# Values of two heads in one block of 512 columns: a projection's blocks are widened in a fused two-branch layer

## The chip, the cores and the metric

The kernel runs on one core of one Trainium2 chip. The metric is the device time of one execution, in microseconds (us), as the median of several runs. The engines are named as the profile names them: PE (TensorE, matmuls; PEld is its weight loads), DVE (VectorE), ACT (ScalarE), POOL (GpSimd), SP (SyncE, which issues most transfers).

## The reference, cut to what matters

The layer has 1024 positions of width 1024. The input is normalised and modulated to `h`, and one projection of `h` gives everything that the two branches need:

```python
h = rms_norm(x, norm_w[l]) * (1.0 + scale[:, None, :]) + shift[:, None, :]
proj = h @ w_in[l]
hq, hf, hi, hz, gq, gk, gv, gz, ga, mg = jnp.split(proj, IN_OFFSETS, axis=-1)
y_h = hgrn2_branch(hq, hf, hi, hz, lb_all[l], hgrn_norm_w[l])
y_g = gla_branch(gq, gk, gv, gz, ga, gla_alpha_w[l], gla_alpha_b[l], gla_norm_w[l])
...
merged = mg[:, :, 0] * u_h + mg[:, :, 1] * u_g
x = x + gate[:, None, :] * (merged @ w_out[l])
return rms_norm(x, final_norm_w)
```

`gla_branch` (the first branch in the kernel) has 4 heads with keys of width 128 and values `gv` of width 256. Each head is a causal linear attention with a decay per key channel, followed by a norm over the head's 256 values and a gate `silu(gz)`. `hgrn2_branch` (the second) has 8 heads of 128. All products are wanted at nearly full float32 precision.

## The kernel before, in words

Matrix products run on operands split in two rounded halves (`hi`, `lo`, made by one ACT copy, L196, and one DVE subtraction, L197), with three matmuls for each product: hi x hi, hi x lo and lo x hi. `h` is kept as eight pairs of tiles 128x1024 (`h_hi`, `h_lo`), columns by positions.

The middle of the program is a list of jobs (`Stream.jobs`), each one block of the input projection. A `Feat` job makes 128 columns of the projection, channels on the partitions (48 matmuls of 512 positions, L541): the gates z, some keys k, and the second branch's q and f. A value job makes positions on the partitions: its stationary operand is 128 positions of `h`, and the moving one is the weights. `Vblk` (L566) makes the 256 value columns of one first-branch head: 192 matmuls of 256 columns (L600 to L602), evicted in two pieces of 128x1024. `Vblk2` (L610) makes 512 columns: 192 matmuls of 512 (L643 to L645), evicted in four pieces. Before the change only the second branch uses `Vblk2`, where 512 columns are four heads.

`Stream.go` runs the jobs in order. A job yields after each unit of work: a `Feat` job 8 times (6 matmuls each), `Vblk` 16 times (12 each), `Vblk2` 32 times (6 each). After every unit `weave` advances two side tracks by fixed amounts: the heads' attentions (`side`, one after another, first in first out) and a back track (`back`: factors and weight sums for the last products, later the output gate). In this way the order of a head's matmuls among the projection's is set by counts of units. `Stream.ahead` loads the weights of up to two jobs ahead and splits those of one job ahead, as far as free buffers allow. Buffers are 46 slots of 128x1024 (`Slots`), taken and given back in turn; a transfer into a slot waits on the chip until the slot's last reader is done, and SP works its queue in order. The back track starts a weight sum only when 12 slots are free (L1185).

A first-branch head (`attention`, L657) makes its scores in three groups on PE (L683; L715; L770, L776, L781) into one PSUM tile, with DVE work between them; then it transposes the keys (L807), builds running states (L829 and DVE L835), and makes its outputs (L848, L850). A head's attention is put on the side track when its value job is done.

After recording, a scheduler places the instructions on each engine. The jobs of the first branch, before: z, z and values of head 0; the same of head 1; k, z, z and values of head 2; the same of head 3. Then follows the second branch, and then the gated and output products (L1343, L1520).

Of the kernel before, what the change touches and what calls it, by code (L numbers as in the profile page):

```python
# [10 lines left out]
F32R = mybir.dt.float32r  # L11
# [4 lines left out]
P = 128  # L16
D = 1024
T = 1024
KT = D // P
# [5 lines left out]
C_GQ, C_GK, C_GV, C_GZ, C_GA, C_MG = 4096, 4608, 5120, 6144, 7168, 7184  # L25
# [58 lines left out]
def hybrid_trunk_kernel(  # L84
# [6 lines left out]
    nc = tc.nc  # L91
    x2, o2 = x[0], out[0]
    w_in2 = w_in[0]
# [7 lines left out]
    S = Slots(sp, N_SLOTS)  # L101
# [3 lines left out]
    def dtile():  # L105
        cnt[0] += 1
        return ps_d.tile([P, T], F32, tag="d", name=f"pd{cnt[0]}")
# [75 lines left out]
    h_hi = [S.get([T], F32R) for _ in range(KT)]  # L183
    h_lo = [S.get([T], F32R) for _ in range(KT)]
# [6 lines left out]
    def split(src, hi=None, lo=None):  # L191

        if hi is None:
            hi = S.get(list(src.shape[1:]), F32R)
            lo = S.get(list(src.shape[1:]), F32R)
        nc.scalar.copy(hi, src)  # L196
        nc.vector.tensor_sub(lo, src, hi.bitcast(F32))  # L197
        return hi, lo
# [109 lines left out]
    raws = {}  # L308
# [15 lines left out]
    g_state = {}  # L324
# [195 lines left out]
    def load_feat(src, w=P):  # L520

        raw = S.get([KT, P])
        nc.sync.dma_start(raw[:, :, 0:w], src.rearrange("(k p) f -> p k f", p=P))
        return raw, w

    def split_feat(lw):
        raw, w = lw
        hi = S.get([KT, P], F32R)
        lo = S.get([KT, P], F32R)
        split(raw[:, :, 0:w], hi[:, :, 0:w], lo[:, :, 0:w])  # L530
        S.free(raw)
        return hi, lo

    def mm_feat(wt, rhs, ps, w=P):
        hi, lo = wt
        for k in range(KT):
            n = 0
            r_hi, r_lo = rhs(k)
            for a, b in ((hi, r_hi), (hi, r_lo), (lo, r_hi)):
                for th in range(2):  # L540
                    nc.tensor.matmul(ps[0:w, th * 512:(th + 1) * 512], a[:, k, 0:w],  # L541
                                     b[:, th * 512:(th + 1) * 512],
                                     start=(k == 0 and n == 0), stop=(k == KT - 1 and n == 2))
                n += 1
            yield

    class Feat:

        raws, parts = 1, 2

        def __init__(self, src, rhs, done, w=P):
            self.src, self.rhs, self.done, self.w = src, rhs, done, w

        def load(self):
            self.lw = load_feat(self.src, self.w)

        def prep(self):
            self.wt = split_feat(self.lw)

        def run(self):  # L560
            ps = dtile()
            yield from mm_feat(self.wt, self.rhs, ps, self.w)
            S.free(*self.wt)
            self.done(ps)

    class Vblk:  # L566

        raws, parts = 2, 4

        def __init__(self, col, done):  # L570
            self.col, self.done = col, done

        def load(self):
            self.raw = []
            for kk in range(2):
                b = S.get([4, 256])
                nc.sync.dma_start(b, w_in2[kk * 512:(kk + 1) * 512, self.col:self.col + 256].rearrange(
                    "(k p) f -> p k f", p=P))
                self.raw.append(b)

        def prep(self):
            self.wt = []
            for b in self.raw:
                hi = S.get([4, 256], F32R)
                lo = S.get([4, 256], F32R)
                split(b, hi, lo)
                self.wt.append((hi, lo))
                S.free(b)

        def run(self):  # L590
            v = [S.get([4, 256]) for _ in range(2)]
            for g in range(2):
                ps = dtile()
                for i in range(4):
                    t = g * 4 + i
                    for k in range(KT):
                        hi, lo = self.wt[k // 4]
                        lh, ll = h_hi[k][:, t * P:(t + 1) * P], h_lo[k][:, t * P:(t + 1) * P]
                        o = ps[:, i * 256:(i + 1) * 256]
                        nc.tensor.matmul(o, lh, hi[:, k % 4, :], start=(k == 0), stop=False)  # L600
                        nc.tensor.matmul(o, lh, lo[:, k % 4, :], start=False, stop=False)  # L601
                        nc.tensor.matmul(o, ll, hi[:, k % 4, :], start=False, stop=(k == KT - 1))  # L602
                        if k % 4 == 3:
                            yield
                nc.scalar.copy(v[g].rearrange("p a b -> p (a b)"), ps)
            for hi, lo in self.wt:
                S.free(hi, lo)
            self.done(v)

    class Vblk2:  # L610

        raws, parts = 4, 8
# [16 lines left out]
                S.free(b)  # L629

        def run(self):
            v = [S.get([2, 512]) for _ in range(4)]
            for g in range(4):
                if g == 2:
                    self.middle()
                ps = dtile()
                for i in range(2):
                    t = 2 * g + i
                    o = ps[:, i * 512:(i + 1) * 512]
                    for k in range(KT):  # L640
                        hi, lo = self.wt[k // 2]
                        lh, ll = h_hi[k][:, t * P:(t + 1) * P], h_lo[k][:, t * P:(t + 1) * P]
                        nc.tensor.matmul(o, lh, hi[:, k % 2, :], start=(k == 0), stop=False)  # L643
                        nc.tensor.matmul(o, lh, lo[:, k % 2, :], start=False, stop=False)  # L644
                        nc.tensor.matmul(o, ll, hi[:, k % 2, :], start=False, stop=(k == KT - 1))  # L645
                        if k % 2:
                            yield
                nc.scalar.copy(v[g].rearrange("p a b -> p (a b)"), ps)
            for hi, lo in self.wt:
                S.free(hi, lo)  # L650
            self.done(v)
# [257 lines left out]
    J = stream.jobs  # L909


    alphas = {}
# [36 lines left out]
    def silu_done(store, key):  # L949
        def f(ps):  # L950
            s = S.get([T])
            nc.scalar.activation(s, ps, AF.Sigmoid)
            nc.vector.tensor_mul(s, s, ps)
            store[key] = s
        return f
# [13 lines left out]

    def gla_attention(h):  # L970
        qk = g_state
        v = qk.pop(("v", h))
        g = {}
        sq = {}

        def post(vh, half, po):
            if half == 0:
                g[vh] = qk.pop(("z", h, vh))
                sq[vh] = S.get([T])
            sl = slice(half * 512, half * 512 + 512)  # L980
            nc.scalar.activation(sq[vh][:, sl], po, AF.Square)
            nc.vector.scalar_tensor_tensor(g[vh][:, sl], po, vec[:, R_GN + vh:R_GN + vh + 1],
                                           g[vh][:, sl], ALU.mult, ALU.mult)

        yield from attention(qk.pop(("q", h)), qk.pop(("k", h)), alphas[h], lambda: v, 0, 256, post)
        S.free(*v)
        nc.gpsimd.tensor_add(sq[0], sq[0], sq[1])
        yield 1.5
        rst = sq[1]
        yield from inverse_root(rst, sq[0], 256)  # L990
        for half in range(4):
            sl = slice(half * 256, half * 256 + 256)
            for vh in range(2):
                nc.vector.tensor_mul(g[vh][:, sl], g[vh][:, sl], rst[:, sl])
            yield 1.5
        for vh in range(2):
            put_act(yg_d, 2 * h + vh, g[vh])
        S.free(*sq.values())

    def gla_k_done(h):  # L1000
        def f(ps):
            t = S.get([T])
            nc.vector.tensor_copy(t, ps)
            g_state[("k", h)] = t
        return f

    def col(c0, w=P):
        return w_in2[:, c0:c0 + w]

    def start_side(gen, wait=1):  # L1010
        stream.side.append([gen, wait])

    class First:
        raws, parts = 0, 0
# [13 lines left out]
                yield  # L1028

    J.append(First())  # L1030
    for h in range(4):
        if h >= 2:
            J.append(Feat(col(C_GK + h * P), rhs_h, gla_k_done(h)))
        J.append(Feat(col(C_GZ + h * 256), rhs_h, silu_done(g_state, ("z", h, 0))))
        J.append(Feat(col(C_GZ + h * 256 + P), rhs_h, silu_done(g_state, ("z", h, 1))))

        def v_done(v, h=h):
            g_state[("v", h)] = v
            start_side(gla_attention(h))
        J.append(Vblk(C_GV + h * 256, v_done))  # L1040

    gate_b = [None]

# [609 lines left out]
    for b in (2, 3):  # L1653
        for p, i, z in ((3, 3, "11"), (6, 1, "21"), (6, 3, "12"), (7, 2, "22")):
            after(b - 1, p, i, lambda b=b, z=z: load_quad(b, z))
            if b == 3:
                p, i = {(3, 3): (7, 2), (6, 1): (7, 3), (6, 3): (4, 2), (7, 2): (4, 3)}[p, i]
# [61 lines left out]
```

## Time and profile before

| | |
|---|---|
| runs | 1215.41, 1216.99, 1218.84 us; median 1216.99 |
| profiled execution | 1216.46 us, of which the span from first to last instruction is 1214.8 us |
| granted TensorE clock | 0.998 of full speed, mean |
| busy share of the span | PE 97%, PEld 81%, DVE 65%, ACT 45%, POOL 10% |
| input-projection weights, `b<-in_w_in_dram` | 66 transfers on SP's queue, 512 KB each, 4.2 us from issue to landing (median) |

In the rows of the profile a line reads: source line, engine, operation, tile written <- tiles read, shape, count | busy us, mean ns of one | idle time before it and what ended it. In the views by stretch each engine has its busy us and, in brackets, its instructions. Matmuls are pipelined, so their busy times overlap; what one costs in a stream is the distance between the starts of two.

### The profile page before, as it was taken

How to read it: one execution, taken by the hardware profiler on the slowest of the kernel's cores; microseconds unless marked ns; L12 is line 12 of the kernel's file. 1: busy time of each engine (PE TensorE's matmuls, PEld its weight loads, DVE VectorE, ACT ScalarE, POOL GpSimd, SP SyncE). 2: the span in 40 equal slices, each digit the busy share in tenths (PEclk: the TensorE clock that was granted, in tenths of full speed). 3: DMA queues.
4: the chain of work that ended last, by engine and by line, in shares of the span. 5: the costliest groups of instructions: out<-in, count | busy, mean ns of one | idle time of the engine just before them, and what ended most of it. 6: DMA issues, size and time to landing. Idle time of an engine off the chain costs nothing.

```text
span 1214.8 us, 20860 instructions
## 1 busy us (share of the span) xinstructions
PE 1184.1 (97%) x8579; PEld 982.6 (81%) x8579; DVE 790.9 (65%) x1245; ACT 546.9 (45%) x797; POOL 123.8 (10%) x215
## 2 busy tenths in 40 slices
PE   5999999999999999999999999999999999999997
PEld 3777889889798888888887888877778888878886
DVE  4637444774848456877884365794653775988994
ACT  5646732434434244344332324455743544444554
POOL 4100000202111121121110101011220000000000
PEclk9999999999999999999999999999999999999999
DMA  9814000844444267255341112054697746435523
GB/s 320 277 70 139 18 19 19 293 141 161 156 152 149 66 207 249 94 179 169 108 174 47 59 53 70 36 174 158 227 343 277 260 160 208 135 104 173 174 104 122
DMA packets 130961, 183.51 MB, mean 151 GB/s; under 512 B 7467, under 2 KB 97633, under 8 KB 130866
## 3 DMA queue, kind: packets, MB, share of 16 engines
q1 hardware_dynamic: 117250, 136.87, 35.7%
q0 software_dynamic: 13568, 45.31, 9.6%
q8 instruction: 67, 1.10, 0.4%
q14 instruction: 28, 0.23, 0.1%
q10 hardware_dynamic: 48, 0.01, 0.0%
HBM read 132.87 MB, written 49.28 MB: 150 GB/s over the span
## 4 chain that ended last, share of the span: by engine, by line
PE 61%; issue 23%; DVE 3%; ACT 3%; POOL 2%; DMA 1%; POOLq 0%; ACTq 0%; DVEq 0%
PE pd L541 19%; PE pd L1343 9%; PE sc_ps L1343 5%; PE pm L1343 5%; PE pd L1520 3%; PE pd L643 2%; PE pd L644 2%; PE pd L645 2%; PE sc_ps L1520 2%; PE pm L848 1%; PE pd L352 1%; PE pm L829 1%; PE pm L850 1%; PE pm L1520 1%; PE sc_ps L352 1%
## 5 line engine op out<-in xcount | busy, mean ns | idle before, releaser
L541 PE MATMUL pd<-b,b 128*128 128x512 f32 x1632 | 387.4, 394 | 0.0
L541 PEld LDWEIGHTS pd<-b,b 128*128 128x128 f32 x1632 | 302.4, 188 | 64.8 <-issue 1.4
L1343 PE MATMUL pd<-b,b 128*128 128x512 f32 x720 | 173.7, 392 | 4.3 <-ACT b L1414 2.1
L1343 PEld LDWEIGHTS pd<-b,b 128*128 128x128 f32 x720 | 133.7, 188 | 35.7 <-ACT b L1414 3.2
L197 DVE TENSOR_TENSOR b<-b,b 128x1024 fp32r<-128x1024 f32 (+2 forms) x89 | 98.9, 1122 | 83.1 <-ACT b L196 65.4
L196 ACT CAST b<-b 128x1024 fp32r<-128x1024 f32 (+2 forms) x89 | 82.9, 948 | 92.1 <-DVE b L1199 14.6
L1286 DVE TENSOR_TENSOR b<-b,b 128x1024 fp32r<-128x1024 f32 x56 | 68.3, 1224 | 66.9 <-ACT b L1285 52.3
L1285 ACT CAST b<-b 128x1024 fp32r<-128x1024 f32 x56 | 58.3, 1050 | 73.9 <-PE pd L1343 20.6
L1343 PE MATMUL sc_ps<-b,b 128*128 128x512 f32 x324 | 79.4, 391 | 1.0 <-ACT scT L793 1.0
L600 PE MATMUL pd<-b,b 128*128 128x256 f32 x256 | 74.2, 290 | 0.0
L1264 DVE TENSOR_TENSOR b<-b,b 128x1024 fp32r<-128x1024 f32 x48 | 59.2, 1251 | 20.8 <-ACT b L1263 15.1
L602 PE MATMUL pd<-b,b 128*128 128x256 f32 x256 | 72.5, 283 | 0.0
L601 PE MATMUL pd<-b,b 128*128 128x256 f32 x256 | 72.4, 283 | 0.0
L1343 PEld LDWEIGHTS sc_ps<-b,b 128*128 128x128 f32 x324 | 60.3, 188 | 14.6 <-ACT scT L793 1.4
L1343 PE MATMUL pm<-b,b 128*128 128x512 f32 x300 | 72.1, 389 | 0.0
L1263 ACT CAST b<-b 128x1024 fp32r<-128x1024 f32 x48 | 49.9, 1050 | 41.2 <-PE pd L1343 16.0
L1343 PEld LDWEIGHTS pm<-b,b 128*128 128x128 f32 x300 | 56.3, 188 | 11.7
L352 PE MATMUL pd<-b,b 128*128 128x512 f32 x192 | 53.3, 410 | 2.0 <-ACT b L196 0.9
L1201 POOL DMA_DIRECT2D ws<-b x64 | 34.6, 541 | 192.0 <-DVE b L1195 86.5
L735 ACT COPY xb<-b 128x512 f32<-128x512 f32 x48 | 29.4, 620 | 49.4 <-PE sc_ps L715 26.7
L643 PE MATMUL pd<-b,b 128*128 128x512 f32 x128 | 51.3, 401 | 0.0
L644 PE MATMUL pd<-b,b 128*128 128x512 f32 x128 | 50.0, 390 | 0.0
(285 smaller groups left out, 1964.3 us busy)
## 6 DMA issues: line engine op xcount, KB each, us to landing
b<-in_w_in_dram SPq DMA_DIRECT2D x66, 512.0 KB, 4.2
ws<-b POOLq DMA_DIRECT2D x64, 256.0 KB, 3.3
b<-ws SPq DMA_DIRECT2D x32, 512.0 KB, 4.9
b<-in_x_dram SPq DMA_DIRECT2D x16, 512.0 KB, 5.7
b<-in_ada_w_dram SPq DMA_DIRECT2D x32, 256.0 KB, 6.9
b<-in_w_branch_dram SPq DMA_DIRECT2D x16, 512.0 KB, 4.4
b<-h SPq DMA_DIRECT2D x14, 512.0 KB, 4.3
wo<-b POOLq DMA_DIRECT2D x14, 512.0 KB, 5.7
```

The lines of the kernel that those rows point to most:

```text
L196: nc.scalar.copy(hi, src)
L197: nc.vector.tensor_sub(lo, src, hi.bitcast(F32))
L352: nc.tensor.matmul(accs[f], wg(a, d, f), b[d][:, half * 512:half * 512 + 512], start=(d == 0 and n == 0), stop=(d == KT - 1 and n == 2))
L541: nc.tensor.matmul(ps[0:w, th * 512:(th + 1) * 512], a[:, k, 0:w], b[:, th * 512:(th + 1) * 512], start=(k == 0 and n == 0), stop=(k == KT ...
L600: nc.tensor.matmul(o, lh, hi[:, k % 4, :], start=(k == 0), stop=False)
L601: nc.tensor.matmul(o, lh, lo[:, k % 4, :], start=False, stop=False)
L602: nc.tensor.matmul(o, ll, hi[:, k % 4, :], start=False, stop=(k == KT - 1))
L643: nc.tensor.matmul(o, lh, hi[:, k % 2, :], start=(k == 0), stop=False)
L644: nc.tensor.matmul(o, lh, lo[:, k % 2, :], start=False, stop=False)
L1286: nc.vector.tensor_sub(lo, t, hi.bitcast(F32))
L1343: nc.tensor.matmul(o, a[:, sl], c, start=(p in (1, 5) and kt == 0 and n == 0), stop=(kt == 3 and n == 2), skip_group_check=True)
L1520: nc.tensor.matmul(o, a, b, start=(p in (1, 5) and kt == 0 and n == 0), stop=(kt == 3 and n == 2), skip_group_check=True)
```

## The change

`Vblk` goes away. The first branch's values are made by `Vblk2`, 512 columns for two heads at a time, and the jobs stand in a new order: z, z of head 0; values of heads 0 and 1; z, z of head 1; k, z, z of head 2; values of heads 2 and 3; k of head 3; z, z of head 3. The attention of the first head of a pair is put on the side track by `middle`, when half of the value block is done; that of head 1 when the block is done, that of head 3 when its keys are done. The attention reads the values as a column offset into the pair's four tiles, which are given back after the pair's second head. `Vblk2` takes each of its four value tiles when it gets to it, no longer all at its start.

```diff
         def run(self):
-            v = [S.get([2, 512]) for _ in range(4)]
+            v = []
             for g in range(4):
+                v.append(S.get([2, 512]))
                 if g == 2:
                     self.middle()
...
-        yield from attention(qk.pop(("q", h)), qk.pop(("k", h)), alphas[h], lambda: v, 0, 256, post)
-        S.free(*v)
+        yield from attention(qk.pop(("q", h)), qk.pop(("k", h)), alphas[h], lambda: qk[("v", h // 2)], h % 2 * 256, 256, post)
+        if h % 2:
+            S.free(*qk.pop(("v", h // 2)))
...
-    for h in range(4):
-        if h >= 2:
-            J.append(Feat(col(C_GK + h * P), rhs_h, gla_k_done(h)))
-        J.append(Feat(col(C_GZ + h * 256), rhs_h, silu_done(g_state, ("z", h, 0))))
-        J.append(Feat(col(C_GZ + h * 256 + P), rhs_h, silu_done(g_state, ("z", h, 1))))
-
-        def v_done(v, h=h):
-            g_state[("v", h)] = v
-            start_side(gla_attention(h))
-        J.append(Vblk(C_GV + h * 256, v_done))
+
+    def gla_z(h):
+        for vh in range(2):
+            J.append(Feat(col(C_GZ + h * 256 + vh * P), rhs_h, silu_done(g_state, ("z", h, vh))))
+
+    def gla_v(h):
+        def done(v):
+            g_state[("v", h // 2)] = v
+            if h == 0:
+                start_side(gla_attention(1))
+        J.append(Vblk2(C_GV + h * 256, done, lambda: start_side(gla_attention(h))))
+
+    def last_k(ps):
+        gla_k_done(3)(ps)
+        start_side(gla_attention(3))
+
+    gla_z(0)
+    gla_v(0)
+    gla_z(1)
+    J.append(Feat(col(C_GK + 2 * P), rhs_h, gla_k_done(2)))
+    gla_z(2)
+    gla_v(2)
+    J.append(Feat(col(C_GK + 3 * P), rhs_h, last_k))
+    gla_z(3)
```

What this does to the order of instructions is shown at three places. The first is PE around the first scores of head 0 (`sc_ps`, 32 small matmuls; `pd` are accumulators of the projection). Before:

```order
L541 MATMUL pd_1419<-b_146,b_1258 128x512 x2
L541 MATMUL pd_1419<-b_154,b_1258 128x512 x2
L541 MATMUL pd_1419<-b_146,b_1259 128x512 x2
L683 MATMUL sc_ps<-xb,b_663 32x80 x32
L541 MATMUL pd_1419<-b_147,b_1258 128x512 x2
```

After (the lines of the changed file are numbered 43 lower there: L640 is L683, and L600 to L602 are `Vblk2`'s three matmuls):

```order
L600 MATMUL pd_1332<-b_1164,b_150 128x512
L601 MATMUL pd_1332<-b_1165,b_150 128x512
L602 MATMUL pd_1332<-b_1164,b_158 128x512
L640 MATMUL sc_ps<-xb,b_663 32x80 x32
L600 MATMUL pd_1332<-b_1152,b_143 128x512
```

The scores stand after 36 units of projection work in both: before, 16 of gates, 16 of values and 4 of the next gates; after, 16 of gates and 20 of values.

The second place is DVE in the scores of head 1, where the weights of the next value block are split (L197 on `b_2090` and `b_2092` before, on `b_1898` to `b_1904` after; L1166 are subtractions of the back track, L1003 and L960 evacuate a key block). Before:

```order
L197 TENSOR_TENSOR b_2300<-b_2092,b_2299 128x1024
L1003 COPY b_2088<-pd_2001 128x1024
L710 TENSOR_TENSOR xb<-b_660,tot_726 128x128x4
L690 TENSOR_TENSOR blk<-sc_ps,eye_679 128x256
...
L718 TENSOR_TENSOR tot_726<-tot_726 128x64
L197 TENSOR_TENSOR b_2296<-b_2090,b_2295 128x1024
L719 TENSOR_TENSOR tot_726<-tot_726 128x64
L1166 TENSOR_TENSOR b_2277<-b_2275,b_2277 128x1024
```

After:

```order
L960 COPY b_1896<-pd_1809 128x1024
L197 TENSOR_TENSOR b_1979<-b_1807,b_1978 128x1024
L667 TENSOR_TENSOR xb<-b_660,tot_726 128x128x4
L197 TENSOR_TENSOR b_2104<-b_1900,b_2103 128x1024
L647 TENSOR_TENSOR blk<-sc_ps,eye_679 128x256
...
L197 TENSOR_TENSOR b_2100<-b_1898,b_2099 128x1024
...
L197 TENSOR_TENSOR b_2108<-b_1902,b_2107 128x1024
...
L197 TENSOR_TENSOR b_2112<-b_1904,b_2111 128x1024
```

Two splits and four back-track subtractions stand between the key block's evacuation and the end of the head's second scores before, five splits and no subtraction after.

The third place is PE at the last products of the back track (the output gate's broadcast, `ones`). Before, in the value block of the second branch's head 4:

```order
L644 MATMUL pd_5955<-b_5712,b_150 128x512
L645 MATMUL pd_5955<-b_5711,b_158 128x512
L1062 MATMUL pm_6017<-b_5918,ones 128x512
L1063 MATMUL pm_6017<-b_5919,ones 128x512
L1062 MATMUL pm_6021<-b_5918,ones 128x512
L1063 MATMUL pm_6021<-b_5919,ones 128x512
L643 MATMUL pd_6026<-b_5699,b_143 128x512
```

After, in the columns of a later job:

```order
L541 MATMUL pd_6082<-b_154,b_6031 128x512 x2
L541 MATMUL pd_6082<-b_146,b_6032 128x512 x2
L1033 MATMUL pm_6112<-b_6001,ones 128x512
L1034 MATMUL pm_6112<-b_6002,ones 128x512
L1033 MATMUL pm_6116<-b_6001,ones 128x512
L1034 MATMUL pm_6116<-b_6002,ones 128x512
L541 MATMUL pd_6082<-b_147,b_6031 128x512 x2
```

They stand after 304 units before and after 340 units now, of 400 in all; the heads' own groups keep their units.

More of the change, by code (lines that the diff above doesn't have):

```diff
@@ L564, in run @@
             self.done(ps)
[L566 to L608, printed above, removed]
     class Vblk2:
@@ L971, in gla_attention @@
         qk = g_state
-        v = qk.pop(("v", h))
         g = {}
```

## The prediction

> **What bounds the kernel now.** I read the page first, for shares and clock, then stretches of the span by engine, then who waited for whom on TensorE, and last the timeline of TensorE inside the blocks that the change rewrites.
>
> ```profile
> span 1214.8 us, 20860 instructions
> ...
> PE 1184.1 (97%) x8579; PEld 982.6 (81%) x8579; DVE 790.9 (65%) x1245; ACT 546.9 (45%) x797; POOL 123.8 (10%) x215
> ...
> PEclk9999999999999999999999999999999999999999
> ```
>
> TensorE is busy 97% of the span, and the granted clock is full in all 40 slices. A busy matmul is only a pipelined one, so the next view asks where TensorE stood still.
>
> ```profile
> core 0: us, PE busy (x) PEld busy (x) DVE busy (x) ACT busy (x) POOL busy (x), PEclk, DMA share, GB/s
> ...
> 112.00:138.00 26.00, 26.00 (x105) 19.41 (x104) 14.54 (x17) 13.42 (x14) 0.00 (x0) 1.00 0.07 20
> 138.00:390.00 252.00, 251.33 (x2354) 225.91 (x2353) 153.93 (x271) 106.45 (x144) 29.36 (x43) 1.00 0.40 130
> 390.00:676.00 286.00, 285.31 (x2593) 235.50 (x2592) 194.28 (x354) 104.59 (x164) 40.86 (x60) 1.00 0.44 143
> ...
> 760.00:1000.00 240.00, 235.17 (x1523) 192.85 (x1522) 155.48 (x204) 122.92 (x175) 23.48 (x36) 1.00 0.60 204
> ```
>
> From 138 to 390 us (the first branch's values, gates and heads, which the change rewrites) TensorE is idle 0.7 us in 252, and in the second branch behind it 0.7 us in 286. The 4.8 us that it loses from 760 to 1000 us lie in the last products, which the change doesn't touch. The waits agree:
>
> ```profile
> engine line waited for: us in total, times, longest us
> PE pm L219 <- DVE b L210: 8.3, 4, 4.0
> ...
> PE sc_ps L715 <- DVE tot L718: 0.7, 1, 0.7
> ```
>
> The longest belongs to the start-up transposes; in the rewritten stretch there is one, 0.7 us, of the scores on VectorE. So a microsecond that TensorE saves here comes off the end, unless a new wait takes it, and everything else the change moves matters only if it makes TensorE wait.
>
> **The change, part by part.**
>
> *Fewer, wider matmuls.* A block of one head issues 2 x 4 x 8 x 3 = 192 matmuls of 256 columns; four blocks make 768. A block of two heads issues 4 x 2 x 8 x 3 = 192 of 512 columns; two make 384. The busy means of the page (283 and 390 ns) overlap and can't be multiplied. I take start-to-start times from runs without side work: the head-0 block (three lines, 64 each, so 192), and 72 matmuls of the existing 512-column block of the second branch (three lines, 24 each).
>
> ```profile
> 138.40 0.28 PE L600 MATMUL pd<-b,b 128*128 128x256 f32 x1
> ...
> 161.44 0.40 PE L541 MATMUL pd<-b,b 128*128 128x512 f32 x1
> ```
> ```profile
> 138.38:161.42 23.04, 18.12 (x64) 1.00 0.09 24
> ```
> ```profile
> 429.35 0.39 PE L643 MATMUL pd<-b,b 128*128 128x512 f32 x1
> ...
> 445.76 0.97 PE L683 MATMUL sc_ps<-xb,b 128*32 128x80 f32 x44
> ```
> ```profile
> 429.34:445.75 16.41, 9.34 (x24) 1.00 0.72 243
> ```
>
> (161.44 - 138.40) / 192 = 0.1200 us for 256 columns; (445.76 - 429.35) / 72 = 0.2279 us for 512. Twice 0.1200 is 0.2400, so 0.0121 us go with the instruction and not with its columns. 768 x 0.1200 = 92.2 us now, 384 x 0.2279 = 87.5 us after: **4.7 us less on TensorE**, all of it on the path. The bounds are other 512-column streams of this trace:
>
> ```profile
> 114.03 16.93 PE L541 MATMUL pd<-b,b 128*128 128x512 f32 x72
> 130.81 1.88 PE L927 MATMUL pm<-b,b 128*128 128x512 f32 x4
> ```
> ```profile
> 1201.24 2.88 PE L1520 MATMUL sc_ps<-b,b 128*128 128x512 f32 x12
> 1203.96 2.88 PE L1520 MATMUL pd<-b,b 128*128 128x512 f32 x12
> ```
>
> The gate columns need (130.81 - 114.03) / 72 = 0.2331 us each, the output product 2.72 / 12 = 0.2267. With these the blocks take 89.5 or 87.1 us: a gain of 2.7 to 5.1. I take 4.7, because the run at 0.2279 is the very code that is now used, with the same operands.
>
> The Trainium skill's "TensorE: Matmul & The Clock Gate", section "Back-to-back issue gap", gives N / 2.4 + 2.5 ns for a warm matmul, so it puts only 2.5 ns on the instruction. By it the change would save an estimated 384 x 2.5 ns = 1.0 us. The measured 12.1 ns disagree, and the sum goes by them.
>
> *Where the side work cuts in.* After each foreign group the first matmul comes late:
>
> ```profile
> 195.55 0.47 PE L600 MATMUL pd<-b,b 128*128 128x256 f32 x1
> 195.86 0.28 PE L601 MATMUL pd<-b,b 128*128 128x256 f32 x1
> ```
> ```profile
> 402.41 0.58 PE L643 MATMUL pd<-b,b 128*128 128x512 f32 x1
> 402.83 0.40 PE L644 MATMUL pd<-b,b 128*128 128x512 f32 x1
> ```
>
> That is 0.31 for 0.12 and 0.42 for 0.23: 0.19 us extra either way. Both forms yield 64 times over all heads' values, so the heads' groups stand at the same unit of work before and after (the order shows the first scores after 36 units in both): nothing changes. "Scores in the middle of a block" therefore moves no score; it replaces the gate columns beside it by value columns. Head 3 may start 16 units sooner, but heads run one after another and head 2 ends only then: nothing.
>
> *Evictions, splits, loads.* Eight evictions of 128x1024, eight splits of 128x1024 and 4 MB of weights stay; ACT gets one more table load at 45% busy. All at nothing, as long as they are ready. What changes is that a block's splits come as four together, no longer two:
>
> ```profile
> b<-in_w_in_dram SPq DMA_DIRECT2D x66, 512.0 KB, 4.2
> ```
> ```profile
> L196 ACT CAST b<-b 128x1024 fp32r<-128x1024 f32 x69 | 71.6, 1050 | 91.7 <-DVE b L1199 14.6 <-DMA b<-in_w_in_dram 12.4 <-PE pd L541 11.7
> ```
> ```profile
> L197 DVE TENSOR_TENSOR b<-b,b 128x1024 fp32r<-128x1024 f32 x69 | 86.1, 1255 | 52.7 <-ACT b L196 35.0 <-PE pd L602 6.6 <-DMA yh<-b 6.5
> ```
> ```profile
> 240.00:265.00 25.00, 24.98 (x293) 21.11 (x291) 22.96 (x44) 11.84 (x21) 2.14 (x4) 1.00 0.58 184
> 300.00:330.00 30.00, 29.34 (x356) 23.88 (x355) 25.66 (x54) 11.87 (x19) 6.08 (x12) 1.00 0.56 185
> 615.00:640.00 25.00, 24.90 (x127) 20.96 (x126) 23.70 (x31) 4.67 (x6) 4.65 (x3) 1.00 0.63 221
> 640.00:700.00 60.00, 60.00 (x502) 47.72 (x501) 22.53 (x46) 19.94 (x32) 3.44 (x3) 1.00 0.17 50
> ```
>
> In the second head's scores (240 to 265 us) the order puts five splits on VectorE where there were two, 3 x 1.26 = 3.8 us more; four subtractions of the same shape leave that stretch. VectorE was busy 23.0 of 25 us there with TensorE idle 0.02. The last of the five stands ahead of VectorE's copy of the third scores; those are 3 units ahead of the second block, which reads its last weights 3 units in: at least 6 units of 1.4 us. Cost: 0, at worst the 3.8. In the third head's scores (300 to 330 us) a gate product leaves; the stall of 0.7 us there may go: 0 to 0.7 gained, I count 0.
>
> *The back track.* Weight sums run only while at least 12 buffers are free. Two heads' values and eight weight halves hold more, so the track falls behind: the order puts its last products 36 units (some 50 us) later. It leaves 615-640 us, where VectorE is 95% busy, and ends where VectorE is busy 22.5 of 60 us; 60 units are still left before the sums are read. Cost 0; if the cover were gone, it would be the waits of the last products.
>
> Sum, against the profiled execution's own 1216.46 us (span 1214.8): 1216.46 - 4.7 = 1211.8. That execution lies 0.5 below the median of the runs, 1216.99, so the median becomes **1212.3 us**, 0.39% less. A measurement of this kernel can tell about 0.3%, 3.7 us, from no change.
>
> **The rivals.**
>
> *Columns alone set the time (no change).* If the 0.0121 us were a property of the second branch's stretch (more DMA traffic: 243 GB/s against 24) and not of the width, the columns, 196,608 before and after, would cost the same: gain 0 to 1, about 1216.5. For it: 512-column streams differ by 3% in this trace for no visible reason. Against: all of them are below 0.2400. The 1.0 us by the Trainium skill's formula above would fall here too. Chance 0.12.
>
> *Weights late (slower).* A two-head block asks for four raw tiles and eight halves at once, and SP's queue is in order: a load that waits for its buffer holds all behind it.
>
> ```profile
> SPq L1189 <- PE pm L829: 40.1, 2, 27.1
> SPq L523 <- PE pm L829: 38.1, 1, 38.1
> ```
>
> Loads do wait on buffers now, up to 38 us, hidden because they are issued up to two jobs ahead. If a buffer is released only as TensorE reaches the job, landing, cast and subtraction are bare: 4.2 + 1.05 + 1.26 = 6.5 us. At one place (second gate columns of head 2, or the second block) that is -4.7 + 6.5 = +1.8, 1218.8, no change by the bound; at both blocks +8.3, 1225.3, slower. It decides once the release comes less than 6.5 us ahead of the use. The nearest that I can read from the order is the second gate columns of head 2, whose cast stands behind work released by the end of the job two before: one job of 48 matmuls, 48 x 0.2331 = 11.2 us, ahead. Chance 0.08 for one place, 0.09 for both.
>
> *VectorE ends last in the second head's scores.* The 3.8 us come through whole: gain 0.9, 1216.1, no change. The 0.02 us of idle now speak against it. Chance 0.06.
>
> **How the numbers follow.** The forecast has the other 0.65. Its own range: gains of 2.7 to 5.8 (5.1 plus the 0.7 stall) give 1214.3 to 1211.2, and the runs (1215.41 to 1218.84) scatter by some 1.7 around their median: 1209.5 to 1216.0. Of the 0.65 I put 0.53 beyond the 3.7 us bound and 0.12 inside. Faster 0.53; same 0.12 + 0.12 + 0.08 + 0.06 = 0.38; slower 0.09. The range reaches to the rivals that change nothing: 1209.5 to 1217.5.
>
> **What would show it.** Right: 384 value matmuls with starts 0.228 us apart in runs without side work; TensorE idle still under 1 us from 112 us to the last products; the first scores about 1 us earlier than now and the last products some 5 us earlier. Wrong: starts at 0.240; TensorE waits on L196 or L197 tiles at the second block or the gate columns ahead of it; or the gain is there at the end of the first branch and lost in the last products.

## The result, and the profile after

The changed kernel takes 1222.62 us, median of 19 runs (1217.12 to 1226.66), against 1216.38 for the kernel before in the same session (1214.69 to 1220.4): ratio 1.0040, 95% interval 1.0030 to 1.0049. It is slower by 0.4%, where 0.39% faster was forecast. The profiled execution took 1220.51 us.

Behind the rewritten class, line numbers are 29 to 43 smaller in the new file: the score groups of a head are L640, L672 and L727 (before L683, L715, L770), `Vblk2`'s matmuls L600 to L602. The page and the stretches of the changed kernel:

```profile
span 1218.8 us, 20087 instructions
...
PE 1183.7 (97%) x8195; PEld 964.5 (79%) x8195; DVE 791.1 (65%) x1245; ACT 548.2 (45%) x798; POOL 121.7 (10%) x215
```
```profile
core 0: us, PE busy (x) PEld busy (x) DVE busy (x) ACT busy (x) POOL busy (x), PEclk, DMA share, GB/s
...
138.00:390.00 252.00, 247.66 (x1967) 206.64 (x1967) 147.60 (x261) 104.93 (x142) 24.44 (x35) 0.99 0.34 109
390.00:676.00 286.00, 283.14 (x2591) 235.47 (x2591) 191.40 (x357) 102.45 (x163) 44.03 (x68) 1.00 0.49 157
676.00:760.00 84.00, 83.74 (x624) 67.64 (x623) 45.30 (x77) 31.12 (x49) 6.87 (x6) 0.98 0.24 68
760.00:1000.00 240.00, 235.19 (x1522) 192.84 (x1521) 157.15 (x206) 122.13 (x174) 23.20 (x36) 1.00 0.59 201
```

The 384 instructions are gone, yet TensorE's busy time has hardly fallen (1184.1 before), in part because some of its work ran at a lower clock (below). In the first branch it is idle 4.3 us of 252 where it was 0.7, in the second 2.9 of 286 where it was 0.7. The waits say for whom:

```profile
engine line waited for: us in total, times, longest us
...
PE sc_ps L672 <- DVE tot L675: 5.4, 2, 4.0
```

One new wait of 4.0 us, at the second score group of head 1. The timelines of ScalarE, VectorE and TensorE just ahead of it (a row begins with its start and its length in us; in brackets stand the idle time of the engine before it and what ended it):

```profile
229.90 1.05 ACT L196 CAST b<-b 128x1024 fp32r<-128x1024 f32 x1 [3.31 <-PE pd L541]
236.50 1.05 ACT L196 CAST b<-b 128x1024 fp32r<-128x1024 f32 x1 [5.54 <-DMA yg<-b]
```
```profile
229.90 1.23 DVE L960 COPY b<-pd 128x1024 f32<-128x1024 f32 x1 [0.50 <-PE pd L541]
237.58 1.22 DVE L197 TENSOR_TENSOR b<-b,b 128x1024 fp32r<-128x1024 f32 x1 [6.46 <-ACT b L196]
238.72 0.68 DVE L667 TENSOR_TENSOR xb<-b,tot 128x512 f32<-128x512 f32 x1
...
241.06 0.42 DVE L647 TENSOR_TENSOR blk<-sc_ps,eye 128x256 f32<-128x256 f32 x1
```
```profile
244.84 0.89 PE L672 MATMUL sc_ps<-xb,b 128*32 128x48 f32 x64 [3.99 <-DVE tot L675]
```

The cast at 236.50 belongs to the last gate columns of head 2. Its weights are there (in experiment 1 below the same cast runs at 218.44), but the buffer for its result is still being read: by the transfer that stores head 0's gated output (`yg<-b`). ScalarE stands 5.54 us; VectorE, whose next instruction is the subtraction of that cast, stands 6.46; all of head 1's score work is queued behind it (in order), and TensorE runs out. From issue to landing the stores took 4.9 to 6.5 us, in a stretch in which the DMA engines were full:

```profile
DMA to landing us min/median/max: 4.9/5.7/6.5
```
```profile
225.00:232.00 7.00, 7.00 (x33) 5.79 (x32) 4.00 (x9) 2.64 (x3) 2.15 (x4) 1.00 0.99 380
```

In the kernel before the same stores took as long, 5.3 to 7.1 us, and no instruction waited for them. So it isn't the slow store that is new; it is who inherits its place.

The stall costs more than its length. The TensorE clock in the stretch behind it, and in one behind the back track's last products (the broadcast with `ones`, called the gate products below):

```profile
246.20:249.60 3.40, 3.40 (x9) 2.64 (x8) 3.30 (x13) 1.70 (x3) 0.00 (x0) 0.50 0.00 0
706.80:710.20 3.40, 3.40 (x9) 2.54 (x9) 0.00 (x0) 0.59 (x1) 0.00 (x0) 0.52 0.00 0
```

Twice the clock is at half speed for 3.4 us: 1.7 us lost each time.

Starts of the same groups of TensorE's work, read from the timelines, as distance from the kernel before (us; the last three columns are experiments told below, with their numbers):

| group | before | after | no hold (1) | held slot (5) | no hold, narrow (6) |
|---|---|---|---|---|---|
| first scores of head 0 | 167.00 | -2.1 | -1.7 | -1.2 | -0.6 |
| first scores of head 1 | 235.64 | -3.1 | -2.7 | -1.2 | -0.8 |
| second scores of head 1 | 243.91 | +0.9 | -2.7 | +3.8 | -0.8 |
| third scores of head 1 | 253.20 | +2.5 | -2.8 | +6.3 | -0.9 |
| first scores of head 3 | 374.12 | -0.3 | -5.6 | +5.8 | +1.7 |
| states, second branch, head 0 | 471.13 | +1.0 | -4.1 | +5.8 | +4.9 |
| second scores, second branch, head 3 | 596.68 | +2.7 | -2.7 | +5.6 | +7.9 |
| last group of the second branch | 854.39 | +5.3 | -2.7 | +6.0 | +7.7 |

Up to 1 us of the first row is the start of the program, which differs from execution to execution. In the changed kernel the blocks do gain (-2.1, then from +2.5 to -0.3); the stall takes 4.1 and the clock 1.5 between the second and the fourth row; the second branch loses 5.6 more, 1.7 of it by the clock behind the gate products. The span ends 4.0 us later.

### The profile page after: what moved, and what is told of

Same layout as the page of the kernel before. It is cut to its first block, busy times and chain, and to the rows that moved or that the text cites. A ratio compares the mean times of both kernels' runs of the same rounds, so it can differ in the third digit from the quotient of the medians.

```text
span 1218.8 us, 20087 instructions
## 1 busy us (share of the span) xinstructions
PE 1183.7 (97%) x8195; PEld 964.5 (79%) x8195; DVE 791.1 (65%) x1245; ACT 548.2 (45%) x798; POOL 121.7 (10%) x215
## 3 DMA queue, kind: packets, MB, share of 16 engines
q8 instruction: 64, 1.05, 0.4%
## 4 chain that ended last, share of the span: by engine, by line
PE 60%; issue 20%; DVE 5%; DMA 4%; ACT 3%; POOL 2%; POOLq 0%; ACTq 0%; DVEq 0%
PE pd L541 18%; PE pd L1314 9%; PE sc_ps L1314 5%; PE pm L1314 5%; PE pd L600 3%; PE pd L602 3%; PE pd L601 3%; PE pd L1491 3%; DMA b<-in_w_in_dram 2%; PE pm L805 2%; PE pm L786 2%; PE sc_ps L1491 2%; PE pm L807 1%; PE pm L1491 1%; PE pd L352 1%
## 5 line engine op out<-in xcount | busy, mean ns | idle before, releaser
L541 PE MATMUL pd<-b,b 128*128 128x512 f32 x1632 | 392.7, 397 | 0.4 <-DVE b L331 0.4
L541 PEld LDWEIGHTS pd<-b,b 128*128 128x128 f32 x1632 | 304.9, 189 | 67.7 <-issue 2.2
L1314 PE MATMUL pd<-b,b 128*128 128x512 f32 x720 | 173.6, 392 | 4.2 <-DVE b L910 2.4
L1314 PEld LDWEIGHTS pd<-b,b 128*128 128x128 f32 x720 | 133.8, 188 | 35.3 <-DVE b L910 2.8
L197 DVE TENSOR_TENSOR b<-b,b 128x1024 fp32r<-128x1024 f32 (+2 forms) x89 | 98.9, 1121 | 72.9 <-ACT b L196 66.0
L600 PE MATMUL pd<-b,b 128*128 128x512 f32 x256 | 102.3, 400 | 0.0
L602 PE MATMUL pd<-b,b 128*128 128x512 f32 x256 | 99.8, 390 | 0.0
L601 PE MATMUL pd<-b,b 128*128 128x512 f32 x256 | 99.8, 390 | 0.0
L602 PEld LDWEIGHTS pd<-b,b 128*128 128x128 f32 x256 | 48.1, 188 | 10.3
L600 PEld LDWEIGHTS pd<-b,b 128*128 128x128 f32 x256 | 48.1, 188 | 10.2
L601 PEld LDWEIGHTS pd<-b,b 128*128 128x128 f32 x256 | 48.1, 188 | 9.5
L352 PE MATMUL pd<-b,b 128*128 128x512 f32 x192 | 53.8, 412 | 1.2 <-ACT b L196 0.9
```

The source lines that it names most:

```text
L352: nc.tensor.matmul(accs[f], wg(a, d, f), b[d][:, half * 512:half * 512 + 512], start=(d == 0 and n == 0), stop=(d == KT - 1 and n == 2))
L1314: nc.tensor.matmul(o, a[:, sl], c, start=(p in (1, 5) and kt == 0 and n == 0), stop=(kt == 3 and n == 2), skip_group_check=True)
```

## Experiments

My theory after the result: a buffer held by a store. Buffers, here also called places or slots, go round in a queue, first in first out, and the fused blocks change who gets which. Rivals: five splits where there were two are simply too much for VectorE (the prediction's third rival), and the width brings nothing.

**1. The held place put last.** One line: when the gate columns of head 2 begin, the place that the store of head 0 still reads goes to the end of the queue of free ones.

```diff
+    stream.hooks[len(J) - 7, 2] = lambda: S.free_list.append(S.free_list.popleft())
     stream.hooks[2, 0] = begin
```

> The changed kernel with one difference: when the gate columns of head 2 have begun, the free buffer whose store of head 0's output may still be in flight is moved to the end of the line of free buffers, so that the split of the next gate columns gets another one. Buffers theory (the split waits for that store, and VectorE's queue waits behind the split): the 4.0 us that TensorE waits at head 1's second scores fall under 0.5, the low clock behind it goes too (some 1.5 us), and the time falls by about 5.5 us from the changed kernel's 1222.6 to 1217. Splits theory (five splits on VectorE instead of two are simply too much work there, 3.8 us): the wait stays at 2 us or more and the time above 1220.

Measured: 1213.49 us (11 runs), ratio to before 0.9975 (0.9966 to 0.9983). It is faster than the kernel before and 9.1 us faster than the change as made, where 5.5 were expected. The matmuls, VectorE's and ScalarE's instructions are as many as in the change, and the five splits are all there. TensorE's order is the same. The scheduler, which plans with the places, now puts this cast six instructions earlier on ScalarE, and two splits ahead of the copy L960 on VectorE. The timelines of ScalarE, VectorE and TensorE:

```profile
218.44 1.05 ACT L196 CAST b<-b 128x1024 fp32r<-128x1024 f32 x1 [1.29 <-DVE b L197]
```
```profile
229.88 1.23 DVE L197 TENSOR_TENSOR b<-b,b 128x1024 fp32r<-128x1024 f32 x1
232.22 1.23 DVE L197 TENSOR_TENSOR b<-b,b 128x1024 fp32r<-128x1024 f32 x1 [1.11 <-ACT b L196]
...
234.50 0.68 DVE L667 TENSOR_TENSOR xb<-b,tot 128x512 f32<-128x512 f32 x1
```
```profile
241.17 0.89 PE L672 MATMUL sc_ps<-xb,b 128*32 128x48 f32 x64
```

The cast runs at 218.44 with no wait for `yg`, 18.1 us sooner, its subtraction at 229.88, and the second scores of head 1 follow without a pause. That speaks against "too many splits": all five are still done between 229 and 251 us, though two of them now stand ahead of L960.

By the changed kernel's own rows the earlier place in the order isn't needed for this. ScalarE is free there at 230.95 (229.90 + 1.05) and VectorE at 231.13, so without the wait for `yg` the subtraction could have begun at some 232.0 instead of 237.58. That is an estimate from these rows: 5.6 us sooner, more than the 3.99 that TensorE stood. (L667 needs the first scores as well; in experiment 1 it runs at 234.50, 4.2 us sooner, which is still more.)

The two profiled executions differ by 7.1 us: 4.0 are the stall, 1.7 the clock behind it, and 1.7 the clock behind the gate products, which stays full here though the same products run (together 7.4). The change's median lies 2.1 us above its profiled execution. No trace shows that part, but the clock has a share in it: the changed kernel's five executions with a mean granted clock of 0.994 took 1224.3 us on average, its four with 0.997 took 1220.5, and nine of experiment 1's eleven have 0.998 or 0.999.

**2. The change with its first-branch blocks in matmuls of 256 columns.** Order and buffers as changed, the width as before.

```diff
-                    o = ps[:, i * 512:(i + 1) * 512]
-                    for k in range(KT):
-                        hi, lo = self.wt[k // 2]
+                    w = 512 // self.pieces
+                    for n in range(KT * self.pieces):
+                        c, k = n // KT * w, n % KT
+                        o = ps[:, i * 512 + c:i * 512 + c + w]
+                        hi, lo = (z[:, k % 2, c:c + w] for z in self.wt[k // 2])
...
```

> The changed kernel, its jobs and buffers, but the first branch's value blocks in matmuls of 256 columns, 768 instead of 384. Cost-per-instruction theory (0.0121 us each whatever the width): 4.7 us slower than the changed kernel, about 1227.3. Columns-alone rival: no difference, 1222.6.

Measured: 1226.65 us (5 runs), ratio 1.0089 (1.0075 to 1.0102): 4.0 us more than the change. The same second scores stall, 3.2 us here:

```profile
PE sc_ps L674 <- DVE tot L677: 6.3, 3, 3.2
```

So width and stall are two things, and the width is worth about what was forecast. The 4.0 also hold a stall that is 0.8 us shorter and one stretch of low clock less than in the change's profile; experiment 6 gives the width alone.

**3. The kernel before with its back track 36 units later.**

```diff
-    stream.back.append([prepare(), 60])
+    stream.back.append([prepare(), 96])
```

> The kernel before, but the back track (factors, weight sums, output gate) begins 36 units later, so that its last products stand after 347 units instead of 304 (340 in the changed kernel). Back-track theory (the some 5 us that the changed kernel loses in the second branch come from this lateness alone): 3 to 5 us slower than before, about 1220. Rival (they come from buffers or from the clock in one profiled execution): within 1 us of before, 1216.4.

Measured: 1219.28 us (11 runs), ratio 1.0023 (1.0014 to 1.0032), 2.9 us more. Its longest new wait is at the second scores of head 2:

```profile
PE sc_ps L715 <- DVE tot L718: 3.2, 2, 2.5
```

The groups shift by +1.9 there and by next to nothing in the second branch. The total is near the theory's 3 to 5 us, but the place isn't: side work that is moved does cost, here in the first branch and not in the second.

**4. and 7. Places with an unfinished store passed over, by rule.** A place freed by an output store is not handed out for the next 8 (experiment 4) or 16 allocations (7).

```diff
-        i = self.free_list.popleft()
+        i = next((j for j in self.free_list if self.stored.get(j, -99) + AWARE < self.serial), self.free_list[0])
+        self.free_list.remove(i)
...
```

> The changed kernel, but a buffer whose store to memory was issued within the last 8 allocations is passed over for as long as another is free, everywhere. If waits of splits on stores in flight are what the changed kernel loses in both branches: 1213 to 1215, the prediction's gain and a little less than before. If only the one place at head 2's gate columns matters: as with the single reordering, about 1217. If buffers are not it: 1222.

Measured with 8: 1220.04 us (7 runs), ratio 1.0034 (1.0022 to 1.0046). The stall is there again, and ScalarE's timeline says why:

```profile
237.30 2.00 ACT L202 CAST b<-b 128x1024 fp32r<-128x1024 f32 x2 [7.37 <-DMA yg<-b]
```

The cast still waits for the store. The rule as written holds a place back for nine allocations. Without it the two places of head 0's stores go to the ninth and the tenth allocation after them; with it they went to the tenth and the eleventh, and those are the two halves of this very split (the next expectation's "ninth" is a miscount).

> As the fourth experiment, but a slot whose last reader is an output store is passed over for the next 16 allocations, not 8 (there the ninth allocation after the store got its slot). Theory of the held slot: the stall at head 1's second scores (3.7 us and 1.5 us of clock) is gone, and the first branch ends some 5 us earlier than before's, as with the slot put last by hand: 1213 to 1215 (other slots change hands too, plus or minus 1). Rival, that the fourth experiment's stall had another cause: 1220 again.

Measured with 16: 1222.70 us (6 runs), ratio 1.0060 (1.0048 to 1.0071). I expected 1213 to 1215 and was wrong. ScalarE and TensorE:

```profile
231.50 2.00 ACT L202 CAST b<-b 128x1024 fp32r<-128x1024 f32 x2 [6.62 <-DMA b<-in_w_in_dram]
234.54 2.00 ACT L202 CAST b<-b 128x1024 fp32r<-128x1024 f32 x2 [1.04 <-DMA yg<-b]
```
```profile
243.24 1.51 PE L678 MATMUL sc_ps<-xb,b 128*32 128x48 f32 x64 [2.39 <-DVE tot L681]
```

Now a cast waits for a weight load first, in the same crowded stretch (the DMA share is 1.0 from 220 to 232 us), and then still 1.04 us for a store. The stall shrinks from 4.0 to 2.4 us, and other places in the program get new ones: 2.5 us at 469, 3.3 at 815. The rule changes every later hand-over; which of them cost was not known ahead.

**5. The held place given to the kernel before.** The opposite test: none of the change, but the place that the second output store still reads is moved to the front as the same gate columns are split.

```diff
+    def held_first():
+        i = S.free_list[4]
+        S.free_list.remove(i)
+        S.free_list.appendleft(i)
+
+    stream.hooks[len(J) - 8, 2] = held_first
```

> The kernel before, value blocks of 256 columns and all, with one line more: when the gate columns of head 2 begin, the place in memory that the second output store of head 0 has just let go of (five allocations down the line) is put first, so that the hi part of the last gate columns of head 2 gets it. No instruction is added, removed or moved in any engine's order. Theory that the changed kernel's stall is a buffer held by a store: the cast on ScalarE waits some 5 us for the store, VectorE's subtraction and the score work of head 1 behind it, TensorE stands 3.3 to 4.0 us at the second score group of head 1 and runs at about 0.78 of its clock for 8 us after (1.5 us): 1216.4 + 5.5 = 1221.9, between 1220 and 1223. Rival, that the stall comes from four splits at a time or from scores that begin in the middle of a block: this kernel has neither, so 1216 to 1217. Rival that only the wait counts and no clock is lost: 1220.2.

In one point this expectation was wrong: the scheduler, which plans with the places, put the cast and its subtraction a few instructions later on their engines, still ahead of head 1's score work. TensorE's order is the same.

Measured: 1222.25 us (5 runs), ratio 1.0047 (1.0035 to 1.0059), 6.3 us more than before. ScalarE, VectorE, TensorE:

```profile
238.56 2.00 ACT L196 CAST b<-b 128x1024 fp32r<-128x1024 f32 x2 [11.70 <-DMA yg<-b]
```
```profile
239.64 1.23 DVE L197 TENSOR_TENSOR b<-b,b 128x1024 fp32r<-128x1024 f32 x1 [6.55 <-ACT b L196]
```
```profile
247.66 1.51 PE L715 MATMUL sc_ps<-xb,b 128*32 128x48 f32 x64 [4.85 <-DVE blk L698]
```

The same chain, in a kernel with splits two by two and with scores at a block's edge: 4.9 us of stall, 2.5 of clock (two dips in a row, 6.8 us at half), and every later group of the table shifted by 5.6 to 6.3 us. So the hand-over of that one place is shown as the cause of the stall from both sides: taken away, the changed kernel is 9.1 us faster (5.7 of them the stall and the clock behind it, by the profiles); put in, the old one is 6.3 slower. No run holds the scheduler's order fixed while the place changes; the rows show the wait, 6.5 us on VectorE in both, and the estimate under experiment 1 says that the wait is enough.

**6. No hold, and 256 columns.** Experiments 1 and 2 together. (The expectation's "768 a block" is the sum of both blocks.)

> The changed kernel without the held slot (as in the first experiment) and with its first value blocks again in matmuls of 256 columns, 768 a block where there are 384. Theory of a price per instruction (12.1 ns, 384 more in two blocks): 1213.5 + 4.7 = 1218.2, all of it inside the two value blocks, and no stall at head 1's second scores. Rival, that time goes by columns alone: 1213.5. Rival, that the gain is given back elsewhere when TensorE arrives earlier (about 2.9 us are, in the second branch): then slowing TensorE by 4.7 costs only some 2 us, 1215.5.

Measured: 1220.90 us (5 runs), ratio 1.0038 (1.0025 to 1.0051): 7.4 more than experiment 1, not 4.7. The price of the instructions is as expected. The first value block up to the first scores, with no score work beside it, in the changed kernel and in this one (matmuls of one of the three lines only):

```profile
137.60:164.90 27.30, 15.57 (x40) 7.32 (x39) 1.00 0.07 20
```
```profile
137.53:166.42 28.89, 22.66 (x80) 14.90 (x79) 1.00 0.07 19
```

3 x 40 instructions in 27.30 us are 0.2275 each, 3 x 80 in 28.89 are 0.1204: 1.59 us for 120 instructions, 13 ns each. In the two blocks that is 384 x 13.2 = 5.1 us. What is beyond that is, in this profile, stalls that experiment 1 hasn't: 1.9 us at 313 and 2.5 at 474, each followed by 1.7 us of low clock. It is the longest of the five executions, 1223.49; three of the others ran at a mean clock of 0.999 against its 0.995, so for the median the excess of 2.3 us is not shown in a trace.

**8. and 9. The second branch's loss.** In experiment 1 the lead falls from 5.6 to 4.1 us at 471. VectorE's timeline there:

```profile
460.84 0.69 DVE L1166 TENSOR_TENSOR b<-b 128x512 f32<-128x512 f32 x1 [2.67 <-DMA b<-in_w_in_dram]
461.45 0.69 DVE L700 TENSOR_TENSOR b<-b,tot 128x512 f32<-128x512 f32 x1
...
465.00 0.69 DVE L1167 TENSOR_TENSOR b<-b,b 128x512 f32<-128x512 f32 x1 [2.06 <-DMA b<-in_w_in_dram]
```

The back track's sums of weights wait for their load, and the scores' work (L700) waits behind them: the in-order queue again. So, on top of experiment 1, experiment 8 lets the sums wait 9 units for their loads, and experiment 9 lets them wait 7 (the edit of 8 is shown).

```diff
-        yield 6
+        yield 9
         s1, s2 = S.get([2, 4, P]), S.get([2, 4, P])
...
```

> The changed kernel without the held slot, and with the side work that adds up weights of the second branch waiting 9 units instead of 6 between its loads and its additions. Theory that the 1.5 us lost at 471 us is VectorE standing 2.7 and 2.1 us for such a load with the scores' work behind it in its queue: those waits go, 1213.5 - 1.4 = 1212.1. Rival, that the load is late because its buffer is (the wait moves with it), or that the later additions and the gate products, now some 50 units later, fall into a worse place: 1213.5 to 1215.

> The changed kernel without the held slot, with the sums of weights waiting 7 units for their loads instead of 6 (the eighth experiment: 9). There the two losses of the second branch before 620 us (1.5 and 1.3 us) were gone, but the side work then ran into scores that it had not met, 1.0 us at 448 and 3.3 us between 762 and 794, near the gate products. Theory that the loads' wait costs time wherever scores stand behind it, and that one unit (some 1.8 us) is enough for most of it, with the gate products at unit 366 instead of 391: 1211.5 to 1213, at or under the first experiment's 1213.5. Rival, that each shift of the side work trades one meeting with scores for another: 1213.5 to 1217.

Measured: 1217.11 us (11 runs), ratio 1.0009 (0.9999 to 1.0020), for 9 units; 1218.79 (12 runs), 1.0019 (1.0009 to 1.0029), for 7. With 9 the losses at 471 and 597 are gone as expected (lead 3.2, 3.1 and 3.7 us at 452, 471 and 597), but 1.0 is lost at 452, and 3.3 between 762 and 794, where the back track now runs into the heads around the gate products. With 7 the lead goes from 5.1 to 0.8 us between 452 and 498, and to nothing at 597. The rival held in both, that each shift trades one meeting for another, and at a higher price than its ranges gave (up to 1215 and 1217). Experiment 1 stays the best version.

## Why the prediction was wrong

- **Fewer, wider matmuls, 4.7 us: right, and a little small.** The same stretch gives 13 ns per instruction, 5.1 us in two blocks; experiment 2 lost 4.0. The 0.2279 us of the sum took in the step to the scores at 445.76: from the first start to that of the last of the 72, at 445.44, it is 16.09 / 71 = 0.2266, and the gain would have come out as 5.2. "Columns alone" is refuted.
  The 2.5 ns of the Trainium skill's "TensorE: Matmul & The Clock Gate" (section "Back-to-back issue gap") do not fit this stream: by them the 120 instructions would have cost an estimated 0.3 us, and 1.59 were measured. That section gives the formula for an isolated matmul and says that in a stream of weight loads and matmuls both set the distance, which the prediction passed over.
- **Where the side work cuts in, 0: right.** The heads' groups keep their places, and with the held place gone the first branch keeps all of the gain (-5.6 at head 3).
- **"Evictions, splits, loads ... all at nothing, as long as they are ready": the step that failed.** The weights were ready; the place for the split was not. Cost: 4.0 us of TensorE and 1.7 of clock. I had the instruction (the second gate columns of head 2) in "weights late", and took its release to be the end of a TensorE job, 11.2 us ahead. The last reader of that buffer was a store whose transfers took 4.9 to 6.5 us to land with the DMA engines full. The release of a buffer has to be read from its last reader, and a transfer is one.
- **"VectorE ends last in the second head's scores": right place, wrong cause.** Five splits instead of two cost no stall there (experiment 1); VectorE stood idle for 6.5 us in the row where I feared it overworked.
- **The back track, 0: wrong by some 3 us.** With the held place gone, 5.6 us of lead at head 3 are 2.7 at the end of the second branch. I looked for a cost only in the last products; it came from sums that wait for loads with scores queued behind (1.5 at 471) and from VectorE being late at 597 (1.3). That the shift by 36 units causes exactly these is not shown: in the old kernel the same shift cost 2.9 us elsewhere.
- **The clock** was in no term, a cost put at nothing without a reason. A stall was priced at its length, and 4.0 us cost 5.5 to 5.7; another 1.7 went behind the gate products.
- A rival with a slower end was there, "weights late", and the time fell between its two prices (1218.8 at one place, 1225.3 at both), with 0.17 between them. That the time lies near it is luck: its mechanism, weights that come late, did not happen. The range ended below.

## What to carry to other kernels

When buffers go round in a queue, a change of tiling also changes who inherits which buffer. Look up, for each instruction that an in-order engine must pass on the way to urgent work, the last reader of the buffer that it writes; a store counts, with its landing time in the busiest stretch. Before judging an idea by the total, put such a hand-over aside with one line: here that turned 1.0040 into 0.9975.

## What the runs showed of the hardware

**A TensorE stall of two or three us can cost 1.7 us more than its length, and where it lies on a grid of 3.41 us decides.** In all eleven profiles, from some 25 us to the last 15, the granted clock is either full or at 0.50. Each dip lasts 3.41 us, which takes 1.7 us off full-speed work, and every stretch at full clock is a whole number of such lengths: 66, 134 and 148 in the changed kernel, 348 in the kernel before. So the clock changes on a grid that doesn't start with the stall (one length of it is called a cell here). Two rows each of the changed kernel and of experiment 7, cut along this grid:

```profile
242.74:246.16 3.42, 1.32 (x66) 1.24 (x67) 3.39 (x9) 0.58 (x1) 0.00 (x0) 1.00 0.51 146
246.16:249.57 3.41, 3.41 (x9) 2.64 (x9) 3.31 (x13) 1.71 (x3) 0.00 (x0) 0.50 0.00 0
```
```profile
813.18:816.59 3.41, 1.82 (x22) 1.10 (x10) 3.41 (x4) 2.18 (x4) 0.00 (x0) 1.00 0.15 60
816.59:820.00 3.41, 1.67 (x7) 1.41 (x8) 3.41 (x7) 0.68 (x2) 0.00 (x0) 1.00 0.00 0
```

In the first pair TensorE is idle 2.1 us of a cell, and the next cell runs at half clock. In the second a longer stall, 3.33 us, falls into two cells with 1.6 and 1.7 us, and the clock stays full. Over all profiles, cells with 2.1 us of idle time or more (seven; the ends of matmuls are modelled) were each followed by a dip, and cells with 1.85 or less by none; of three with 1.89 or 1.90, one was. The stall of 4.84 us, which filled one whole cell, was followed by two dips.

The Trainium skill's "TensorE: Matmul & The Clock Gate" (section "What's actually happening") tells of a free-running window of about 3.4 us after whose idling the clock is halved. The half clock, the 3.4 us and the grid agree with these rows; that a whole window must be idle does not, as 2.1 us were enough.

One dip, behind the two pairs of one-row matmuls among the gate products (706.8 us in the changed kernel), came without a stall. It fits the same count if a matmul of one row is taken as idle time: both pairs, 2.08 us, fell into one cell there, and in experiment 1 into two, 1.05 us each. That rests on one dip and isn't shown further. If so, the 1.7 us behind the gate products are a matter of where the program stands on the grid, and not of the change.

The clock row of the profile's page shows none of this: it reads 9 in all 40 slices for the changed kernel as for the one before, as a slice is some 30 us long.
